# The mixer's output projection by seven products in two chunks

## The chip, the cores and the metric

One core of one Trainium2 chip. The metric is the device time of one execution in microseconds (us), the median over the runs shown, lower is better.

## The reference

One inference step of one hybrid layer, for a prompt of 512 tokens and 8 single sampled tokens, 520 columns in all; everything is float32. What matters here:

```
proj = rmsnorm(x, g_mix) @ w_in          # 2048 -> 6160 columns
ya   = bg * causal_dwconv(cg * hin)      # short convolution: 1024 features
yb   = norm(gla(q, k, v, gate)) * silu(og)   # 4 linear-attention heads: 1024 features
x1   = x + concat([ya, yb]) @ w_out      # 2048 x 2048, the output projection
u, v = split(rmsnorm(x1, g_ffn) @ w_up)  # 2048 -> 2 * 5632
h    = silu(causal_dwconv(u) + b) * v
x2   = x1 + h @ w_down                   # 5632 x 2048
y    = rmsnorm(x2, g_final)
```

## The kernel before, in words

Activations lie with features on the 128 partitions and the T = 520 tokens along the row, in two halves of HT = 260. A float32 operand is split into a rounded part hi (ScalarE, a copy into fp32r) and a rest lo = raw - hi (VectorE), and every product is three matmuls: hi by hi, hi by lo and lo by hi. Weights are streamed from DRAM as 512 KB pieces `raw` of 128x1024, by DMAs on the queue of SP (SyncE), and split the same way into `hi` and `lo`.

The order of work:

1. *Input projection.* Tiles of 128 output columns. `group()` issues, for one tile, 16 rows of weights x 3 x 2 halves of matmuls (L134). Eight tiles of the mixer's convolution branch (`conv_tile`), then four attention heads, and eight tiles of its output gate. Each finished tile of 128 mixer outputs is split into yh and yl, which stay in SBUF (`ym`).
2. *Output projection* (`projected`, `kept`, L914 to L1003). 16 tiles, again by `group()`, in pairs (k, k+8). To each the residual from `xT_d` is added, the result goes to DRAM (`x1_d`), its squares are added up on GpSimd (POOL) in `ssq`, and, multiplied by the norm's weight, it becomes one of the quarters of the FFN's input. From a pair, `quarter_sums` forms four sums of quarters, `t21` and `t34`; these go to DRAM (`t_d`). During the last pair, whose two tiles are interleaved, they come back on SP's queue, and `sums_parts` splits them in place of the mixer's outputs that are no longer needed.
3. *FFN up*, 44 tiles t, and *FFN down*, 5 chunks c of 1024 features x 4 groups g of 512 outputs; the last 512 features are done in the ordinary way. Both use a scheme of seven products in place of the eight quarter products of a 2x2 block multiplication. Each product takes a weight piece or a sum of weight pieces, and a quarter of the input or a sum of quarters (the "input forms"). One product is 24 matmuls of 128x128 by 128x260 in both.
4. Final norm.

Step 3's two stages share one loop over `order`, a list of (kind, where, product): seven products j = 0..6 per tile or group. At each product the loop issues the matmuls, and puts what other engines must do at fixed points of it: `begin(n)` asks for three of the next group's four weight pieces at j = 0, `load_rest` for the fourth at j = 2; `prepare(i + 2)` makes hi and lo (L1093 on ScalarE, L1097 on VectorE) for the product two further on, and a sum of weights (`plus`, L1048, in a single tile `s` that is updated in place: pieces 22 + 21, then + 11, then + 12). The sum for product 7 is an adding DMA from SBUF to SBUF (`seventh`, L1062, the rows raw<-raw) on POOL's queue at j = 5. Steps such as `gate(t)`, which turns a finished up tile into h, are generators: each `yield` says how many products after its start the next part is issued. Engines run their instructions in this order of issue, and so do the DMA queues of SP and POOL.

The FFN's norm factor R (one number per token) is computed from `ssq` at the third product of the first up tile, whose products stand in an order of their own, with more PSUM banks (`BANK0`). The other tiles take R in when PSUM is emptied (`up_finish`).

In the down-projection the input forms of chunk c are read from DRAM (`f_d`, written by `gate`) by `load_form(c, j)`, four DMAs of 128x2x260 for each of the seven products; the forms for chunk 0 are asked for in the last up tile at j = 4 (four products' worth) and in the first down group at j = 0 (three). The residual x1 is read into `acc` (`load_residual`, at j = 6 of the last up tile for group 0). The share of the fifth product that two accumulators need is kept in `h5` and added by POOL in the last chunk.

## Time and profile before

| | |
|---|---|
| Time, median of 3 runs | 2246.64 us (2244.97 to 2248.2) |
| The profiled execution: its own time | 2249.65 us |
| its span, first to last instruction | 2247.9 us |
| TensorE (PE) busy | 2206.9 us, 98% of the span, 18147 matmuls |
| VectorE (DVE) busy | 1559.2 us, 69% |
| ScalarE (ACT) busy | 997.4 us, 44% |
| GpSimd (POOL) busy | 406.6 us, 18% |
| Transfers | 377.09 MB, 168 GB/s on average |
| Mean granted TensorE clock | 0.993 |

All rows but the first come from one profiled execution, and durations in the text are its durations. "Busy" counts the time in which at least one instruction of the engine ran; since matmuls are pipelined, a single matmul's duration (some 283 ns) is longer than the distance from one to the next. The busy share is a mean over the stages named above, which have quite different loads; the stage of the output projection lies at about 688 to 876 us of the span, FFN up at 876 to 1768, and FFN down from there on.

### The profile page before, as it was taken

What the parts mean: (1) busy time and instruction counts of PE and PEld (TensorE: products, weight loads), DVE (VectorE), ACT (ScalarE), POOL (GpSimd) and SP (SyncE); (2) the same over time, 40 slices, a digit from 0 to 9 for tenths busy, and PEclk for the clock granted to TensorE, in tenths of its full rate; (3) what the DMA queues carried; (4) which work ended last, traced back from release to release, by engine and by line L of the source; (5) the groups of instructions that cost most, each with busy time, mean ns of one, the idle gap of its engine ahead of it and who ended that gap; (6) DMA issues with size and microseconds to landing.
All of it is one profiled execution on the core that took longest, in us unless ns stands there. A gap on an engine that the chain in (4) does not pass through costs nothing.

```text
span 2247.9 us, 43792 instructions
## 1 busy us (share of the span) xinstructions
PE 2206.9 (98%) x18147; PEld 2183.9 (97%) x18147; DVE 1559.2 (69%) x2081; ACT 997.4 (44%) x1417; POOL 406.6 (18%) x539
## 2 busy tenths in 40 slices
PE   8999999999999999999999999999999999999997
PEld 6999999999999998999999999999999999999997
DVE  5355363544334547888889888898888767777876
ACT  5334334312222335555555555555555444444445
POOL 3023132210001222111311122112122400000310
PEclk9999999999999999999999999999999999999999
DMA  8243334333444556576776767667676987876944
GB/s 247 83 132 102 111 113 114 99 104 86 109 118 137 163 159 203 151 188 159 184 186 175 185 165 188 177 172 179 175 187 191 302 239 212 264 212 186 285 120 151
DMA packets 459395, 377.09 MB, mean 168 GB/s; under 512 B 19081, under 2 KB 423461, under 8 KB 459053
## 3 DMA queue, kind: packets, MB, share of 16 engines
q1 hardware_dynamic: 429585, 280.03, 43.6%
q0 software_dynamic: 28288, 92.05, 15.7%
q8 instruction: 142, 2.33, 0.4%
q10 hardware_dynamic: 1324, 2.23, 0.3%
q14 instruction: 56, 0.46, 0.1%
HBM read 278.15 MB, written 63.27 MB: 152 GB/s over the span
## 4 chain that ended last, share of the span: by engine, by line
PE 83%; issue 7%; DMA 4%; DVE 3%; POOL 2%; ACT 1%; SPq 0%; ACTq 0%; POOLq 0%; DVEq 0%
PE mm L134 32%; PE mm L1125 22%; PE ms L1125 9%; PE y L1312 6%; PE x L1312 6%; PE f L1312 2%; PE e L1312 2%; PE ms L753 1%; DMA raw<-raw 1%; POOL f_d L1192 1%; DMA raw<-in_w_in_dram 0%; PE ms L739 0%; PE tp L284 0%; DVE lo L106 0%; DVE lo L1097 0%
## 5 line engine op out<-in xcount | busy, mean ns | idle before, releaser
L1125 PE MATMUL mm<-yl,hi 128*128 128x260 f32 x1408 | 398.8, 283 | 0.0
L1125 PE MATMUL mm<-yh,hi 128*128 128x260 f32 x1408 | 397.9, 283 | 0.0
L1125 PE MATMUL mm<-yh,lo 128*128 128x260 f32 x1408 | 397.3, 282 | 0.0
L1093 ACT ACTIVATE hi<-raw 128x1024 fp32r<-128x1024 f32 x256 | 270.7, 1057 | 205.9 <-issue 72.4
L1097 DVE TENSOR_TENSOR lo<-raw,hi 128x1024 fp32r<-128x1024 f32 x256 | 318.6, 1245 | 53.9 <-ACT hi L1093 52.5
L105 ACT ACTIVATE hi<-raw 128x1024 fp32r<-128x1024 f32 x144 | 152.0, 1056 | 394.4 <-PE mm L134 378.5
L134 PE MATMUL mm<-xh,hi 128*128 128x260 f32 (+2 forms) x1280 | 314.1, 294 | 10.1 <-ACT xh L120 5.7
L106 DVE TENSOR_TENSOR lo<-raw,hi 128x1024 fp32r<-128x1024 f32 x144 | 185.6, 1289 | 183.9 <-ACT hi L105 173.6
L1097 DVE TENSOR_TENSOR lo<-s,hi 128x1024 fp32r<-128x1024 f32 x192 | 238.0, 1239 | 101.1 <-ACT hi L1093 95.9
L134 PE MATMUL mm<-xh,lo 128*128 128x260 f32 (+2 forms) x1280 | 302.0, 285 | 0.7 <-DVE lo L106 0.7
L134 PE MATMUL mm<-xl,hi 128*128 128x260 f32 (+2 forms) x1280 | 299.7, 283 | 1.5 <-DVE xl L121 1.4
L1093 ACT ACTIVATE hi<-s 128x1024 fp32r<-128x1024 f32 x192 | 202.8, 1056 | 177.8 <-DVE s L1048 58.2
L1125 PEld LDWEIGHTS mm<-yh,lo 128*128 128x128 f32 x1408 | 265.5, 189 | 0.0
L1125 PEld LDWEIGHTS mm<-yl,hi 128*128 128x128 f32 x1408 | 265.0, 188 | 0.0
L1125 PEld LDWEIGHTS mm<-yh,hi 128*128 128x128 f32 x1408 | 264.6, 188 | 0.0
L134 PEld LDWEIGHTS mm<-xh,hi 128*128 128x128 f32 x1280 | 216.5, 190 | 20.3 <-issue 7.7
L134 PEld LDWEIGHTS mm<-xl,hi 128*128 128x128 f32 x1280 | 216.4, 190 | 2.3 <-DVE xl L121 2.3
L134 PEld LDWEIGHTS mm<-xh,lo 128*128 128x128 f32 x1280 | 215.0, 189 | 1.1 <-DVE lo L106 1.1
L1125 PE MATMUL ms<-xh,hi 128*128 128x260 f32 x704 | 199.9, 284 | 2.8 <-ACT xh L117 2.8
L1125 PE MATMUL ms<-xh,lo 128*128 128x260 f32 x704 | 199.7, 284 | 0.0
L1125 PE MATMUL ms<-xl,hi 128*128 128x260 f32 x704 | 199.1, 283 | 0.5 <-DVE xl L118 0.5
L1062 POOL DMA_DIRECT2D raw<-raw x63 | 56.4, 895 | 594.5 <-DVE s L1048 503.5
(397 smaller groups left out, 5242.9 us busy)
## 6 DMA issues: line engine op xcount, KB each, us to landing
raw<-in_w_up_dram SPq DMA_DIRECT2D x176, 512.0 KB
raw<-in_w_down_dram SPq DMA_DIRECT2D x96, 512.0 KB
raw<-in_w_in_dram SPq DMA_DIRECT2D x92, 512.0 KB
form<-f_d SPq DMA_DIRECT2D x126, 260.0 KB
raw<-raw POOLq DMA_DIRECT2D x63, 512.0 KB, 5.5
f_d<-t POOLq DMA_DIRECT2D x80, 260.0 KB, 5.5
raw<-in_w_out_dram SPq DMA_DIRECT2D x28, 512.0 KB
f_d<-fh POOLq DMA_DIRECT2D x40, 260.0 KB, 4.9
```

The source lines that it names most:

```text
L105: nc.scalar.activation(hi, raw, AF.Copy)
L106: nc.vector.tensor_tensor(lo, raw, hi.bitcast(F32), op=ALU.subtract)
L134: nc.tensor.matmul(o, w, xx, start=first and i == 0, stop=last and i == 2)
L753: nc.tensor.matmul(pb[:, c * 64 : (c + 1) * 64], L[:, c, :], rhs[:, c], start=True, stop=True,)
L1062: nc.gpsimd.dma_start(raw[2, 1], raw[1, 1], accum_op=ALU.add)
L1093: nc.scalar.activation(his[i], src, AF.Copy)
L1097: nc.vector.tensor_tensor(los[i], src, his[i].bitcast(F32), op=ALU.subtract)
L1125: nc.tensor.matmul(st["bank"][b], w[:, k, :], x, start=b not in st["used"] and k == 0 and j == 0, stop=k == 7 and j == 2, skip_group_check ...
L1192: nc.gpsimd.dma_start(d, x)
L1312: nc.tensor.matmul(ps[:, m, :], w[:, k, m * P : (m + 1) * P], x, start=b not in st["used"] and k == 0 and j == 0, stop=k == 3 and j == 2, ...
```

## The change

The output projection joins the loop of seven products. `order` now begins with 2 chunks c x 4 groups g of kind "wo": chunk c stands for half of the 2048 mixer features, group g for 512 of the 2048 outputs, and `chunk_product` and `chunk_finish` (before: `down_product`, `down_finish`) serve them as they serve the down-projection.

- *Its inputs.* A mixer tile isn't split on its own: with every second tile (`mixed_done`) the sums of quarters are made (`pair_sums`), and four tiles are split and stored to DRAM (`g_d`) as hi and lo, by eight DMAs on POOL's queue (`stored`). `load_form("wo", c, j)` reads them back on POOL's queue: chunk 0 during the last output-gate tiles, chunk 1 mostly during the last group of chunk 0.
- *Its results* are added up in `acc`, into which `load_residual` first reads the residual from `xT_d`.
- *The FFN's inputs.* In chunk 1, the group's four accumulators become final during the group. `projected(g)` then stores them (`ready`, to `x1_d`, on SP's queue), scales them, squares them (`square`; the sums `ssq` are adding DMAs on POOL's queue), and makes quarters and sums of quarters, split into place (`form`) or, for groups 0 to 2 and the forms 4, 5 and 6, into temporary tiles and from there to `t_d` (`out`, on SP's queue), whose home still holds inputs of the output projection. `load_sum` reads these back on SP's queue in the last group.
- *Weight sums.* In chunk 1 the third sum of a group is an adding DMA as well (`dma_plus`, with `dma[3]` issued at j = 0).
- *R* is computed in the second up tile, from `norm_sums`; the first two up tiles have it multiplied in afterwards, and `gate(0)` starts five products later. All up tiles now use one order of products.
- *Down.* The fifth product's share goes directly into the accumulators at r = 6 (`onto`), and `h5` is gone. The forms for chunk 0 are asked for in the last up tile at j = 1, 2, 4 and 6, and the residual at j = 5.
- Pools: the tiles of the input in SBUF are laid out in pairs (`pair_tiles`), and the weight pieces of the second column have a pool of their own (`raw2`).

```diff
+    g_d = [dp.tile([7, 2, 4, P, HT], F32, name=f"g_d{c}") for c in range(2)]
+    t_d = dp.tile([3, 4, 2, P, T], F32, name="t_d")
...
+    def load_form(kind, c, j):
+        home = (7 * c + j) % 8
+        parts_ = []
+        for x in range(2):
+            tiles = []
+            for q in range(2):
+                t = slots[2 * home + q].tile(
+                    [P, T], F32R, tag=f"y{'hl'[x]}{2 * home + q}", name="form"
+                )
+                first = kind == "wo" or c == 0 and x == 1
+                (nc.gpsimd if first else nc.sync).dma_start(
+                    two(t.bitcast(F32)),
+                    forms_d[kind][c][PLACE[ORDER[j]], x, 2 * q : 2 * q + 2].rearrange(
+                        "i p c -> p i c"
+                    ),
+                )
+                tiles += halves(t)
+            parts_.append(tiles)
+        xd[kind, c, ORDER[j]] = list(zip(*parts_))
+    def stored(src, dst, hi):
+        hi = hi[:, : src.shape[1]]
+        split(src, hi.bitcast(F32R), src.bitcast(F32R))
+        for d, x in zip(dst, (hi, src)):
+            if len(d.shape) == 3:
+                x = two(x)
+                d = d.rearrange("f p c -> p f c")
+            nc.gpsimd.dma_start(d, x)
+    def pair_sums(he, h):
+        t21, t34 = tmp()[:, :T], tmp()[:, :T]
+        (b11, b12), (b21, b22), (t2, t1), (t3, t4) = map(halves, (he, h, t21, t34))
+        sub(t1, b11, b12)
+        minus(t2, t1, b22)
+        sub(t3, b22, b12)
+        minus(t4, t2, b21)
+        return t21, t34
...
+        def mixed_done(k, y):
+            if k % 2 == 0:
+                return
+            he, dst, i = even.pop(k - 1), g_d[k // 8], k // 2 % 4
+            t21, t34 = pair_sums(he, y)
+            for src, f in ((halves(he)[0], 6), (t21, 0), (t34, 2), (y, 4)):
+                n = 1 if f == 6 else 2
+                stored(src, [dst[f : f + n, x, i] for x in range(2)], tmp())
...
+            if 2 <= j < 6:
+                for x in range(2 * j - 4, min(2 * j - 2, 7)):
+                    load_form("wo", 0, x)
...
-        def kept(m, xt):
-            nc.gpsimd.dma_start(x1_d[m], xt[:, :T])
-            if m == 0:
-                nc.scalar.activation(ssq, xt[:, :T], AF.Square)
-            else:
-                sq = tmp()
-                nc.scalar.activation(sq[:, :T], xt[:, :T], AF.Square)
-                ptt(ssq, ssq, sq[:, :T], ALU.add)
...
-        for k in range(LK):
-            for m in (k, k + 8):
-                xt = tmp()
-                nc.sync.dma_start(xt[:, :T], xT_d[m])
-                projected(m, group(w_out, m * P, ya), xt)
-                kept(m, xt)
-            t21, t34 = tmp()[:, :T], tmp()[:, :T]
-            quarter_sums(k, t21, t34)
-            nc.gpsimd.dma_start(t_d[k], t21)
...
-                if k % 8 < LK:
-                    load_sums(k)
...
+        def dma_plus(out, x):
+            return lambda: nc.gpsimd.dma_start(out, x, accum_op=ALU.add)
...
+        sums = {5: plus(s, raw[2, 2], raw[2, 1]), 6: plus(s, s, raw[1, 1])}
+        dma = {}
+        if state:
+            dma[7] = dma_plus(raw[2, 1], raw[1, 1])
+        else:
             sums[7] = plus(raw[2, 1], raw[2, 1], raw[1, 1])
-        def seventh():
-            nc.gpsimd.dma_start(raw[2, 1], raw[1, 1], accum_op=ALU.add)
-        return dict(src=src, sums=sums, bank={}, used=set(), rest=loads[3], seventh=seventh)
...
+    groups = [("wo", (c, g)) for c in range(2) for g in range(NG)]
+    groups += [("up", (t,)) for t in range(NF)]
+    groups += [("down", (c, g)) for c in range(NCD) for g in range(NG)]
+    order = [(*x, r) for x in groups for r in ORDER]
+    NW = 7 * 2 * NG
+    NU = NW + 7 * NF
...
+        if r == 2 and t < 2:
+            nc.scalar.activation(z1, bk["e"], AF.Copy)
         elif r == 2:
             nc.vector.tensor_tensor(z1, bk["e"], R[:, :HT], op=ALU.mult)
-        elif r == 7:
-            add(v2, bk["a"], st["c"])
         elif r == 3:
             add(z2, bk["f"], st["c"])
-            nc.vector.tensor_tensor(z2, z2, R[:, HT:], op=ALU.mult)
-        elif r == 4:
...
+        d = 0 if t else 5
+        yield d
+        nc.vector.tensor_tensor(v[:, :T], v[:, :T], R, op=ALU.mult)
+        yield d + 0.5
+        if t < 2:
+            nc.vector.tensor_tensor(z[:, 2 : 2 + T], z[:, 2 : 2 + T], R, op=ALU.mult)
         c = tmp()
...
-                ptt(acc[g, 1], acc[g, 1], h5[g], ALU.add)
-                ptt(acc[g, 3], acc[g, 3], h5[g], ALU.subtract)
+        if r == 6:
+            onto(1, "c")
+            onto(3, "c", ALU.subtract)
...
+    def form(f, g):
+        if f == 1:
+            x = pair_tiles(bigA, f"b{g}")
+        elif f in (2, 3):
+            x = [
+                bigA.tile([P, T], F32R, tag=acc_tag(4 * g + q), name="b2")
+                for q in ((0, 3) if f == 2 else (1, 2))
+            ]
+        else:
+            k = {5: 0, 4: 4, 6: 8, 7: 12}[f] + g
+            x = [slots[k].tile([P, T], F32R, tag=f"y{s}{k}", name=f"y{s}{k}") for s in "hl"]
+        for j, q in enumerate(zip(*(halves(y) for y in x))):
+            xq[f, 2 * g + j] = q
+        return x
+    def projected(g):
+        xg = {}
+        def ready(q):
+            a, m = acc[g, q], first_tile("wo", g, q // 2)
+            nc.sync.dma_start(rows_of(x1_d, "wo", g, q), two(a))
+            xg[q] = tmp()[:, :T]
+            for j in range(2):
+                nc.scalar.activation(
+                    halves(xg[q])[j], halves(a)[j], AF.Copy, scale=gffn[:, m + j : m + j + 1]
+                )
+        def square(q):
+            if g == 0 and q in (0, 3):
+                nc.scalar.activation(ssq[q % 2], acc[g, q], AF.Square)
+                return
+            sq = fh()
+            nc.scalar.activation(sq, acc[g, q], AF.Square)
+            nc.gpsimd.dma_start(ssq[q % 2], sq, accum_op=ALU.add)
+        def out(f, t):
+            if f == 7 or g == NG - 1:
+                split(t, *form(f, g))
+            else:
+                hi = tmp()[:, :T]
+                split(t, hi.bitcast(F32R), t.bitcast(F32R))
+                for d, x in zip((t_d[f - 4, g, 0], t_d[f - 4, g, 1]), (hi, t)):
+                    nc.sync.dma_start(d, x)
+        yield 4.5
+        ready(0)
+        split(xg[0], *form(1, g))
+        yield 5.5
+        ready(3)
+        square(0)
+        yield 6.5
+        ready(1)
+        square(3)
+        yield 7
+        t1, t2 = xg[0], tmp()[:, :T]
+        sub(t1, xg[0], xg[1])
+        minus(t2, t1, xg[3])
+        yield 7.5
+        ready(2)
+        out(5, t1)
+        yield 8
+        t4 = tmp()[:, :T]
+        minus(t4, t2, xg[2])
+        yield 8.5
+        out(4, t2)
+        out(7, t4)
+        yield 9
+        square(1)
+        split(xg[2], *form(2, g))
+        t3 = xg[1]
+        sub(t3, xg[3], xg[1])
+        yield 9.5
+        out(6, t3)
+        yield 10.5
+        square(2)
+        yield 11
+        split(xg[3], *form(3, g))
+    def load_sum(f, g):
+        for x, d in zip(form(f, g), (t_d[f - 4, g, 0], t_d[f - 4, g, 1])):
+            nc.sync.dma_start(x.bitcast(F32), d)
...
+            if kind == "wo" and at[0] == 1:
+                steps.append([projected(at[1]), i, 0])
...
+        if j == 0 and 3 in state[kind, at]["dma"]:
+            state[kind, at]["dma"][3]()
+        if j == 5 and more:
+            state[groups[n + 1]]["dma"][7]()
...
-        if i == 2:
-            factors = rsqrt_rest(rsqrt_sums(ssq), D, R)
-        if i in (3, 4):
+        if i == NW + 7:
+            factors = rsqrt_rest(norm_sums(), D, R)
+        if i in (NW + 8, NW + 9):
             next(factors)
-        if kind == "up" and n == NF - 1:
-            if j == 4:
-                for x in range(4):
-                    load_form(0, x)
-            if j == 6:
-                load_residual(0)
+        if kind == "wo":
+            c, g = at
+            if c == 0 and g == 0 and j == 0:
+                load_form("wo", 1, 0)
+            if c == 0 and j == 4 and g + 1 < NG:
+                load_residual("wo", g + 1)
+            if c == 0 and g == NG - 1 and j >= 1:
+                load_form("wo", 1, j)
+            if c == 1 and g == NG - 1:
+                for f, h in {
+                    1: ((5, 0), (5, 1)), 2: ((5, 2),), 3: ((4, 0), (4, 1)), 4: ((4, 2),),
+                    5: ((6, 0), (6, 1)), 6: ((6, 2),),
+                }.get(j, ()):
+                    load_sum(f, h)
+        if kind == "up" and at[0] == NF - 1:
+            for x in {1: (0, 1), 2: (2, 3), 4: (4, 5), 6: (6,)}.get(j, ()):
+                load_form("down", 0, x)
+            if j == 5:
+                load_residual("down", 0)
...
-            if c == 0 and g == 0 and j == 0:
-                for x in (4, 5, 6):
-                    load_form(0, x)
...```

What this does to the order of instructions, at three places. First VectorE. Before, in the output projection, while the next to last pair's results are finished (mm is what the matmuls left in PSUM, t a temporary tile, xl the rest of a split quarter, lo the rest of a weight piece):

```order
L106 TENSOR_TENSOR lo<-raw,hi 128x1024
L924 TENSOR_TENSOR t<-mm,t 128x260 x2
L106 TENSOR_TENSOR lo<-raw,hi 128x1024
L917 TENSOR_TENSOR t<-t 128x260
L919 TENSOR_TENSOR t<-t 128x260
L118 TENSOR_TENSOR xl_8102<-t,xh_8101 128x520
L918 SCALAR_TENSOR_TENSOR t<-t 128x260
L920 SCALAR_TENSOR_TENSOR t<-t 128x260
```

and after, in a group of the second chunk (acc<-acc,y is an accumulator's update, s a weight sum):

```order
L1032 TENSOR_TENSOR s<-s,raw 128x1024
L1263 TENSOR_TENSOR acc<-acc,y 128x520
L589 TENSOR_TENSOR t<-t 128x520
L583 SCALAR_TENSOR_TENSOR t<-t 128x520
L1087 TENSOR_TENSOR lo<-s,hi 128x1024
L118 TENSOR_TENSOR t<-t 128x520
L583 SCALAR_TENSOR_TENSOR t<-t 128x520
L1087 TENSOR_TENSOR lo<-raw,hi 128x1024
L118 TENSOR_TENSOR t<-t 128x520
L118 TENSOR_TENSOR yl_9172<-t,yh_9171 128x520
L118 TENSOR_TENSOR b_9204<-t,b_9203 128x520
```

Between two weight pieces there now stand accumulators' updates, weight sums and several sums and splits of the FFN's inputs, where one pair's sums and one split stood.

Second, SP's queue at the end of the output projection. Before, the last weights of w_out, the first of w_up, and then the sums of quarters from DRAM:

```order
L983 DMA raw<-in_w_out_dram 128x4x128 x2
L1045 DMA raw<-in_w_up_dram 128x8x128 x3
L1076 DMA raw<-in_w_up_dram 128x8x128
L978 DMA t<-xT_d 128x520 x2
L955 DMA t<-t_d 128x520 x12
```

and after:

```order
L1308 DMA x_d<-acc 128x2x260 x3
L1029 DMA raw<-in_w_up_dram 128x8x128 x3
L1308 DMA x_d<-acc 128x2x260
L1331 DMA t_d<-t 128x520 x4
L1369 DMA yh_9461<-t_d 128x520
L1369 DMA yl_9462<-t_d 128x520
L1369 DMA yh_9465<-t_d 128x520
L1369 DMA yl_9466<-t_d 128x520
L1066 DMA raw<-in_w_up_dram 128x8x128
L1331 DMA t_d<-t 128x520 x2
```

The stores of the results and of the sums of quarters have moved onto this queue, between the weights and ahead of the loads of the same sums.

Third, POOL's queue where the down-projection begins. Before, the forms for chunk 0 (on this queue the half with x = 1, the lo parts), with the adding copy of weights between them:

```order
L1266 DMA form<-f_d_9504 128x2x260 x8
L1062 DMA raw<-raw 128x1024
L1280 DMA acc<-x_d 128x2x260 x4
L1266 DMA form<-f_d_9504 128x2x260 x6
L570 DMA out_dram<-flat 11x128 x10
L1192 DMA hh_d_9515<-fh 128x520
L1192 DMA hl_d_9516<-t 128x520
```

and after:

```order
L612 DMA form<-f_d_7543 128x2x260 x8
L630 DMA hh_d_7552<-fh 128x520
L630 DMA hl_d_7553<-t 128x520
L612 DMA form<-f_d_7543 128x2x260 x4
L1036 DMA raw<-raw 128x1024
L1220 DMA acc<-x_d 128x2x260 x4
L612 DMA form<-f_d_7543 128x2x260 x2
L574 DMA out_dram<-flat 11x128 x10
L630 DMA hh_d_7554<-fh 128x520
```

Twelve forms instead of eight stand ahead of the copy, but the first eight are issued two to three products earlier, and a store of the last tiles' h stands between them.

More of the change, by code (lines that the diff above doesn't have):

```diff
@@ L1072, in begin @@
         kind, at = groups[n]
-        state[at] = weights(up_source if kind == "up" else down_source, *at)
+        state[kind, at] = weights(source(kind, at), kind == "wo" and at[0] == 1)
     def load_rest(n):
-        nc.sync.dma_start(*state[groups[n][1]]["rest"])
+        nc.sync.dma_start(*state[groups[n]]["rest"])
     def prepare(i):
@@ L1242, in gate, with fh @@
         yield 14
-        stored(h, [dst[4:6, x, i] for x in range(2)])
+        stored(h, [dst[4:6, x, i] for x in range(2)], fh())
+    def fh():
+        return wxp.tile([P, T], F32, tag="fh", name="fh")
     f_d = [dp.tile([7, 2, 4, P, HT], F32, name=f"f_d{c}") for c in range(NCD)]
+    forms_d["down"] = f_d
     hl_d = [[dp.tile([P, T], F32, name=f"h{s}_d{t}") for s in "hl"] for t in range(CH)]
@@ L1351, in down_finish @@
             onto(2, "a", ALU.subtract)
+    ssq = [cp.tile([P, T], F32, tag="glr", name="ssq"), R]
+    def form(f, g):
[6 more added lines that the diff above has]
+            ]
+        else:
+            k = {5: 0, 4: 4, 6: 8, 7: 12}[f] + g
[3 more added lines that the diff above has]
+        return x
@@ L1355, in run_steps, with norm_sums @@
+    def load_sum(f, g):
+        for x, d in zip(form(f, g), (t_d[f - 4, g, 0], t_d[f - 4, g, 1])):
+            nc.sync.dma_start(x.bitcast(F32), d)
+    def norm_sums():
+        pss = []
+        for b in range(2):
+            pss.append(bank())
+            for j, x in enumerate(halves(ssq[b])):
+                nc.tensor.matmul(pss[b][:, :HT], ones, x, start=j == 0, stop=j == 1)
+        return pss
     def run_steps(now):
@@ L1380, in trunk_kernel @@
             seeded = {b: two_banks(b) for b in "ef"}
[L1381 to L1389 removed]
+        elif i == NW:
+            mmp = pctx.enter_context(tc.tile_pool(name="mm", bufs=4, space=PSUM))
+            msp = pctx.enter_context(tc.tile_pool(name="misc", bufs=4, space=PSUM))
@@ new lines, in trunk_kernel @@
+        (up_product if kind == "up" else chunk_product)(i)
+        if j == 0:
+            if n and groups[n - 1][0] == "up":
+                steps.append([gate(groups[n - 1][1][0]), i, 0])
+            if kind == "wo" and at[0] == 1:
+                steps.append([projected(at[1]), i, 0])
+        run_steps(i)
+        if i in (0, NU):
+            marked(seeded["e"], xd[kind, 0, 1][0][0])
+        if i in (2, NU + 2):
+            marked(seeded["f"], xd[kind, 0, 1][0][0])
+        if i == NW:
+            x = xq[1, 0][0]
+            for ps in [bank() for _ in range(4)]:
+                nc.tensor.matmul(ps[:, :HT], x[:, :P], x, start=True, stop=True)
```

356 lines of the change are left out of this document (117 added, 239 removed).

## The prediction, made before the changed kernel was run

> **What bounds the kernel now.** I read the page's parts 1 and 2 first, then the same stretches as a table by stage, then the groups of instructions.
>
> ```profile
> PE 2206.9 (98%) x18147; PEld 2183.9 (97%) x18147; DVE 1559.2 (69%) x2081; ACT 997.4 (44%) x1417; POOL 406.6 (18%) x539
> ...
> PEclk9999999999999999999999999999999999999999
> DMA  8243334333444556576776767667676987876944
> ```
>
> TensorE is busy for 98% of the span at full clock; nothing else is near that. So time goes only where matmuls go, or where TensorE starts to wait. The stages (columns: start:end, length, then busy us and count for PE, PEld, DVE, ACT, POOL, then PEclk, DMA share, GB/s) show how much room the other engines have:
>
> ```profile
> 600.00:684.00 84.00, 84.00 (x701) 84.00 (x700) 32.26 (x43) 24.39 (x29) 0.00 (x0) 1.00 0.41 115
> 690.00:840.00 150.00, 150.00 (x1252) 150.00 (x1251) 69.24 (x89) 48.00 (x65) 30.48 (x37) 1.00 0.51 160
> 920.00:1720.00 800.00, 800.00 (x6674) 800.00 (x6673) 710.43 (x953) 434.34 (x641) 157.84 (x227) 1.00 0.68 177
> 1840.00:1870.00 30.00, 30.00 (x253) 30.00 (x252) 21.95 (x22) 13.05 (x15) 0.87 (x1) 1.00 1.05 327
> 1870.00:1900.00 30.00, 30.00 (x253) 30.00 (x252) 22.79 (x24) 12.65 (x14) 1.71 (x2) 1.00 0.68 188
> ```
>
> The rows are the end of the input projection, the output projection, the FFN's up-projection and two pieces of its down-projection. 1252 matmuls in 150 us are 119.8 ns each; that pitch is the same in all five. VectorE at 89% (row three) and the transfers at 1.05 and 327 GB/s (row four) are the highest loads that still cost TensorE nothing. There are two places where it does wait, the crossing from the output projection into the FFN and that from up to down:
>
> ```profile
> 872.00:880.00 8.00, 4.67 (x24) 4.28 (x23) 7.97 (x15) 5.38 (x10) 4.73 (x4) 0.79 0.37 115
> ...
> 892.00:896.00 4.00, 1.97 (x17) 1.79 (x16) 3.55 (x6) 1.76 (x2) 3.83 (x3) 1.00 0.62 159
> ```
>
> ```profile
> 1760.00:1770.00 10.00, 8.35 (x58) 7.95 (x57) 8.84 (x12) 3.62 (x5) 8.13 (x12) 0.87 1.01 348
> 1770.00:1780.00 10.00, 10.00 (x82) 10.00 (x81) 3.88 (x4) 5.57 (x9) 5.08 (x9) 0.96 1.06 322
> 1780.00:1790.00 10.00, 9.08 (x76) 8.87 (x75) 8.57 (x10) 3.71 (x4) 7.33 (x14) 1.00 1.07 353
> 1790.00:1800.00 10.00, 10.00 (x85) 10.00 (x85) 5.54 (x6) 3.22 (x4) 6.36 (x9) 1.00 1.07 352
> 1800.00:1810.00 10.00, 7.83 (x51) 7.42 (x50) 4.85 (x6) 4.25 (x5) 0.00 (x0) 0.83 1.02 319
> ```
>
> At 119.8 ns, 12 us hold 100 matmuls; the first pair of rows has 41, so 59 are missing: 7.1 us. 50 us hold 417; the second table has 352: 65 x 0.1198 = 7.8 us.
>
> **The change part by part.** *Matmuls.* The output projection is 16 tiles x 16 rows of weights x 3 x 2 halves:
>
> ```profile
> L134 PE MATMUL mm<-yh,hi 128*128 128x260 f32 x512 | 103.5, 284 | 0.0
> L134 PE MATMUL mm<-yh,lo 128*128 128x260 f32 x512 | 103.3, 283 | 0.0
> L134 PE MATMUL mm<-yl,hi 128*128 128x260 f32 x512 | 102.6, 281 | 0.0
> ...
> L517 PE MATMUL ms<-ssq,ones 128*128 128x260 f32 x4 | 1.0, 382 | 0.0
> ```
>
> That is 1536. After: 2 chunks x 4 groups x 7 products x 24 = 1344, of the same shape. 192 fewer x 0.1198 = **-23.0 us**. Four marking matmuls (0.5 us) and two more sums over ssq are added (today's two are the four records of L517, 1.0 us): **+1.5**.
>
> *The old crossing.* The 59 matmuls were missing because the last two tiles' split, sums and t_d loads stood on VectorE (busy 7.97 of 8 us) with TensorE waiting, and then for R's factors. After, the inputs of the first FFN tile come with each group, and the first two tiles do without R: **-7.1** for what goes; what comes in its place is priced next.
>
> *VectorE in the second chunk.* From the groups (mean ns), and the timeline, where ops that follow each other start closer than their durations:
>
> ```profile
> L1097 DVE TENSOR_TENSOR lo<-raw,hi 128x1024 fp32r<-128x1024 f32 x256 | 318.6, 1245 | 53.9 <-ACT hi L1093 52.5 <-DMA form<-f_d 1.4
> L1048 DVE TENSOR_TENSOR s<-s,raw 128x1024 f32<-128x1024 f32 x128 | 156.6, 1223 | 2.2
> L118 DVE TENSOR_TENSOR yl<-t,yh 128x520 fp32r<-128x520 f32 x32 | 21.8, 695 | 11.4 <-ACT yh L117 11.3
> L1326 DVE TENSOR_TENSOR acc<-acc,e 128x520 f32<-128x520 f32 x20 | 13.9, 693 | 0.9
> ```
>
> ```profile
> 865.80 1.91 DVE L118 TENSOR_TENSOR yl<-t,yh 128x520 fp32r<-128x520 f32 x3
> 867.63 1.22 DVE L1048 TENSOR_TENSOR s<-raw 128x1024 f32<-128x1024 f32 x1
> ...
> 884.94 1.21 DVE L1097 TENSOR_TENSOR lo<-raw,hi 128x1024 fp32r<-128x1024 f32 x1
> 886.07 1.21 DVE L1048 TENSOR_TENSOR s<-s,raw 128x1024 f32<-128x1024 f32 x1
> ```
>
> So 1.13 us apart for the wide ones, 0.61 (1.83 / 3) for 520 columns. A group of the second chunk has 7 lo and 2 weight sums (9 x 1.13 = 10.2), 6 additions onto acc, 4 input sums and 7 splits (17 x 0.61 = 10.4): 20.6 us, against 168 x 0.1198 = 20.1 for TensorE. Over four groups it falls 2 us behind; weights are made two products (5.8 us) ahead, so this may cost nothing (low end 0). By the full durations it is 9 x 1.24 + 17 x 0.69 = 22.9, so 4 x 2.8 = 11 (high end). The pitch was seen on this engine in full flow, so I stand near it but add a little for its waits on ScalarE: **+3**. ScalarE's share is smaller:
>
> ```profile
> L1093 ACT ACTIVATE hi<-raw 128x1024 fp32r<-128x1024 f32 x256 | 270.7, 1057 | 205.9 <-issue 72.4 <-PE mm L1125 61.1 <-PE x L1312 19.6
> L117 ACT ACTIVATE yh<-t 128x520 fp32r<-128x520 f32 x32 | 19.9, 636 | 29.8 <-DVE t L603 10.4 <-DVE t L900 10.4 <-DMA t<-t_d 7.8
> L1179 ACT ACTIVATE t<-mm 128x260 f32<-128x260 f32 x43 | 16.7, 389 | 80.4 <-PE mm L1125 80.4
> ```
>
> 7 x 1.06 + 13 x 0.64 (7 splits, 4 squares, 2 copies) + 8 x 0.39 = 18.9 of 20.1: full, but not over, and its overlap is not counted.
>
> *Transfers in the second chunk.* Sizes are from the list of DMA issues:
>
> ```profile
> raw<-raw POOLq DMA_DIRECT2D x63, 512.0 KB, 5.5
> f_d<-fh POOLq DMA_DIRECT2D x40, 260.0 KB, 4.9
> x_d<-t POOLq DMA_DIRECT2D x16, 260.0 KB, 2.4
> t_d<-t POOLq DMA_DIRECT2D x14, 260.0 KB, 3.6
> ```
>
> A middle group moves four weight pieces (2.1 MB), two adding copies raw<-raw (1.05), 4 x1_d stores, 4 adding copies onto ssq and 6 t_d stores (14 x 0.266 = 3.7): 6.9 MB. The first has no t_d and no ssq copies yet but 2.5 MB left of the 24 form loads issued in the group before: 6.4. In the last group and the five FFN products until the last t_d tile is used, 12 products or 34.5 us, it is 18 t_d loads (4.8), the weights and copies of two groups and what is left of the stores: 12 MB. Together 6.4 + 6.9 + 6.9 + 12 = 32.2 MB in 3 x 20.1 + 34.5 = 94.8 us. At 353 GB/s (row 1780) that takes 91 us: nothing (low end). At 188 / 0.68 x 1.07 = 295, which is row 1870's mix of weights, copies and forms run at the share's top, 109: +14 (high end). The mix lies between, with more plain 260 KB pieces than row 1870, so I take 325: 99 us, **+4.3**. The waiting places: t_d loads stand on SP's queue behind t_d and x1_d stores that wait for VectorE and ScalarE, and ahead of the next weights, which have 20 us in hand; ScalarE's split into a new tmp waits for a t_d store two products old (landing 3.6 us where nothing was crowded, so 2 us spare); the third weight sum is now a POOL copy behind the form loads, with three products for its 5.5 us.
>
> The Trainium skill, *DMA: Bandwidth & Descriptors*, section "Specifications", gives about 358 GB/s as the HBM limit of a core. The busiest row here, 353, agrees. Copies from SBUF to SBUF (7.4 of the 32.2 MB) would not count there, so by the page the stretch would need an estimated 69 us, the term would be 0 and the sum 4.3 us lower.
>
> *Mixer and start of the projection.* A pair of tiles gets four small sums, two more splits, 8 stores of 1.9 MB on POOL. At 600 to 684 VectorE is at 38%, ScalarE at 29%, transfers at 115 GB/s, POOL empty: hidden; earlier POOL also runs the heads' steps, and 8 issues (some 0.6 us each) can delay one. The first chunk's forms load during the last tiles; the first three products' weights are ready before these end. On VectorE the evacuation, four sums and four splits of the last pair then stand between weights: about 8 us for what must be ready in 8.6. Between 0 and one product (2.9): **+0.5**. The adding copies replace 15 additions on POOL, each free before.
>
> *R's factors* come in the second FFN tile; between 0 and the 2 us lost at 892 to 896: **+1**.
>
> *The crossing to the down-projection.* Now the forms load from the second product of the last FFN tile on, not from the fifth, some 8.6 us earlier, and no longer ahead of the adding copy of weights in one lump. The chain of waits shows what was late:
>
> ```profile
> 1767.66 9.37 DMA raw<-raw
> 1779.25 6.51 DMA form<-f_d
> 1786.04 5.11 DMA out_dram<-flat
> 1794.56 7.86 DMA raw<-raw
> ```
>
> The bytes are the same and the second group's copy still stands behind forms, ten small stores and residuals, so not all of the 7.8 us goes: ends -7.8 and 0, I take **-4**. One addition more per down group (0.61 us in rows with VectorE at 73 to 76%) is hidden; so are eight POOL additions that go.
>
> **Sum.** -23.0 + 1.5 - 7.1 + 3 + 4.3 + 0.5 + 1 - 4 = -23.8. The profiled execution took 2249.65 us (span 2247.9 and 1.75 around it): 2225.85. It lies 3.0 above the median of the runs, 2246.64, against which I predict: 2222.85, said as **2223**.
>
> **The rivals.** (1) *The second chunk is bound by its transfers* (slower). Row 920 to 1720, with weights, one adding copy per tile and form stores, moved 177 GB/s at a share of 0.68: 260 at a full share. If doubled adding copies hold it to 250, 32.2 MB take 129 us, 34 more than TensorE instead of 4.3: 2223 + 30 = 2253. It decides from about 262 GB/s downwards, where the sum is zero. For it: the adding copies are a fifth of the bytes, and no row shows them this dense. Against: weights come here in pieces twice as wide as in that stage, and 1840 to 1870 reached 327 without loss. (2) *VectorE sets the pace*, by full durations and each of its waits on ScalarE: +11 instead of +3, so 2231. For it: VectorE is above the 89% that is known to be free. Against: the pitch. (3) *The transfers never bind*, 353 GB/s holding at both places: terms 4.3 and -4 become 0 and -7.8, 2215. This is what the Trainium skill's limit above gives for the first of the two. For it: the 30 us at 327. Against: 1800 to 1810, where one late copy cost 34 matmuls, 4 us. (4) *No change*: several of these terms at middling values, 2242 to 2251. That the matmuls are not removed is excluded: the program has 190 rows fewer on TensorE.
>
> **How the numbers follow.** Forecast 0.55 (2216 to 2234 by itself), (1) 0.10, (2) 0.15, (3) 0.15, (4) 0.05. Low end: all of (3) and no VectorE loss, 2211 or so; high end: (2) with the transfers at 295, 2223 + 8 + 10 = 2241, and a little of (4): 2244. That leaves out (1) and the edges of (3) and (4), under 0.2. 0.2% (4.5 us) is about what a measurement of this kernel can tell from no change. Faster by more: forecast, (2), (3), 0.85; within: 0.05; slower: 0.10.
>
> **What would show it.** In the new profile, 8 groups of 20.1 us at pitch 119.8 ns in the output projection; VectorE close to full in the second half of it; GB/s above 300 there; the first FFN tile without a hole like 872 to 880; the crossing to down with fewer than 65 missing matmuls. I am wrong if matmuls in the second chunk come in under 150 per 20 us, or if the hole of the old crossing is back under another name, such as a split waiting for a t_d load.

## The result, and the profile after

2262.64 us, median of 4 runs (2257.99 to 2263.39), against 2246.81 for the kernel before: 15.8 us slower, ratio 1.0067, 95% interval 1.0049 to 1.0084. I had forecast 2223 and a range of 2211 to 2244. The profiled execution took 2262.26 us, its span is 2260.6, 12.7 above before.

Parts 1 and 2 of the page after:

```profile
PE 2195.8 (97%) x17963; PEld 2172.9 (96%) x17963; DVE 1631.3 (72%) x2188; ACT 1039.6 (46%) x1486; POOL 461.4 (20%) x640
...
PE   8999999999999977999999999999999999999997
...
DMA  8343354374787789476676766667666987876944
GB/s 249 84 126 105 107 156 113 87 210 121 201 248 242 219 233 299 126 195 174 167 195 160 194 173 178 183 160 193 174 180 191 308 236 218 258 205 195 282 122 151
```

There are 184 fewer matmul records (192 matmuls fewer for the projection, 8 more for sums and markings), and yet TensorE's share of the longer span is lower: two slices at 7 tenths, from about 790 to 905 us, where before stood 9. By stage (after, then the same stretches before; a 25 us stretch without gaps has 210 records, since a stretch also counts those that overlap its ends):

```profile
690.00:770.00 80.00, 80.00 (x667) 80.00 (x666) 63.51 (x66) 33.74 (x37) 32.84 (x46) 1.00 0.84 254
770.00:795.00 25.00, 21.02 (x151) 20.51 (x150) 14.66 (x18) 11.90 (x19) 3.78 (x5) 0.86 0.64 178
795.00:930.00 135.00, 109.92 (x837) 108.40 (x836) 93.16 (x111) 78.37 (x121) 24.95 (x26) 0.90 0.90 243
930.00:1720.00 790.00, 787.57 (x6572) 787.29 (x6572) 703.66 (x946) 428.90 (x632) 154.06 (x221) 1.00 0.67 176
```

```profile
770.00:795.00 25.00, 25.00 (x210) 25.00 (x210) 10.92 (x14) 8.26 (x11) 4.95 (x6) 1.00 0.51 160
795.00:930.00 135.00, 129.65 (x1060) 128.94 (x1059) 91.23 (x117) 63.08 (x89) 27.95 (x26) 0.99 0.59 173
```

The first chunk (row 690) loses nothing. From 770 to 930, the second chunk and the start of the FFN, there are 988 matmuls against 1270 before: 282 missing, 33.8 us more than before. A further 2.4 us is lost in row 930, where before had none: VectorE multiplies R into the second up tile afterwards, a step of ScalarE waits for that, and behind this step stands the copy of a PSUM bank that TensorE needs. That is nearly the whole result: -23.0 for the products, +33.8 and +2.4 here, about 13 against the spans' 12.7 (changes of 1 us and less are left out).

Who waited, in that stretch, by the lists of waits of TensorE and ScalarE (total us, times, longest):

```profile
PE y L1249 <- ACT f L1269: 11.2, 2, 6.1
PE x L1249 <- ACT f L1269: 7.4, 1, 7.4
```

```profile
ACT t L117 <- DMA t_d<-t: 26.7, 3, 10.1
```

and the same on ScalarE's and SP's timelines and on the chain of waits:

```profile
798.95 1.04 ACT L1083 ACTIVATE hi<-raw 128x1024 fp32r<-128x1024 f32 x1
807.80 0.64 ACT L117 ACTIVATE t<-t 128x520 fp32r<-128x520 f32 x1 [7.82 <-DMA t_d<-t]
808.35 0.59 ACT L1269 ACTIVATE f<-y 128x520 f32<-128x520 f32 x1
```

```profile
791.07 3.17 SPq L1029 DMA_DIRECT2D raw<-in_w_out_dram  x3
794.33 1.19 SPq L1308 DMA_DIRECT2D x_d<-acc  x1
795.61 3.76 SPq L1331 DMA_DIRECT2D t_d<-t  x4
799.47 0.42 SPq L1066 DMA_DIRECT2D raw<-in_w_out_dram  x1
```

```profile
763.45 9.97 DMA form<-g_d
...
773.98 7.76 DMA s<-raw
...
799.06 9.23 DMA t_d<-t
...
826.60 11.57 DMA t_d<-t
...
877.18 10.85 DMA x_d<-acc
...
894.03 7.06 DMA x_d<-acc
```

Five holes, and a transfer at the start of each. The split for sum 6 needs a ninth temporary tile out of a ring of eight, and gets that of sum 5. The store of that tile is the first of the four t_d stores in SP's row. It left at 795.6, just after ScalarE had made the tile, with three pieces of weights and a store of x1 still on their way ahead of it. The semaphore on which the split waits was full 12.1 us later, and the split starts at 807.8. (The chain's rows name the last of the four stores instead, 799.06 and 826.60, and so show 9.23 and 11.57.) In the next two groups this store took 12.7 and 8.0 us. ScalarE stands still for it three times, with the copy of a PSUM bank (`f`) behind it, for which TensorE waits. The first hole begins with the adding copy s<-raw behind the form loads on POOL's queue, the last with the split that overwrites an accumulator: it waits for the store of x1, which stands among 18 loads of sums. After each hole the granted clock is low for a while:

```profile
785.00:790.00 5.00, 5.00 (x26) 5.00 (x26) 4.48 (x6) 4.54 (x8) 0.86 (x1) 0.54 0.31 107
790.00:795.00 5.00, 5.00 (x45) 5.00 (x44) 4.93 (x7) 3.59 (x8) 0.01 (x1) 1.00 0.91 199
```

26 matmuls instead of 44 in a fully busy 5 us: 18 x 0.12, another 2.2 us for this hole. (The Trainium skill, *TensorE: Matmul & The Clock Gate*, "What's actually happening", has the clock at half after an idle window of some 3.4 us; the rows agree, 0.54 after a hole of about 4 us.)

### The profile page after: what moved, and what is told of

Read it like the earlier page. It is cut to its first block, busy times and chain, and to the rows that moved or that the text cites. A ratio compares the mean times of both kernels' runs of the same rounds, so it can differ in the third digit from the quotient of the medians.

```text
span 2260.6 us, 43939 instructions
## 1 busy us (share of the span) xinstructions
PE 2195.8 (97%) x17963; PEld 2172.9 (96%) x17963; DVE 1631.3 (72%) x2188; ACT 1039.6 (46%) x1486; POOL 461.4 (20%) x640
## 2 busy tenths in 40 slices
PE   8999999999999977999999999999999999999997
DMA  8343354374787789476676766667666987876944
## 4 chain that ended last, share of the span: by engine, by line
PE 88%; DMA 6%; DVE 3%; ACT 1%; POOL 1%; issue 1%; SPq 0%; ACTq 0%; DVEq 0%; POOLq 0%
PE mm L1108 27%; PE mm L134 25%; PE ms L1108 11%; PE y L1249 8%; PE x L1249 8%; PE f L1249 3%; PE e L1249 3%; PE ms L830 1%; DMA t_d<-t 1%; DMA form<-g_d 1%; DMA x_d<-acc 1%; DVE lo L1087 1%; DMA raw<-in_w_down_dram 0%; DMA acc<-x_d 0%; PE ms L1516 0%
## 5 line engine op out<-in xcount | busy, mean ns | idle before, releaser
L1083 ACT ACTIVATE hi<-raw 128x1024 fp32r<-128x1024 f32 x288 | 304.4, 1057 | 225.7 <-issue 79.5
L1108 PE MATMUL mm<-yh,hi 128*128 128x260 f32 x1408 | 398.6, 283 | 2.8 <-ACT ms L1118 2.4
L1108 PE MATMUL mm<-yl,hi 128*128 128x260 f32 x1408 | 397.8, 283 | 0.0
L1108 PE MATMUL mm<-yh,lo 128*128 128x260 f32 x1408 | 397.5, 282 | 0.0
L1087 DVE TENSOR_TENSOR lo<-raw,hi 128x1024 fp32r<-128x1024 f32 x288 | 351.3, 1220 | 57.7 <-ACT hi L1083 57.6
L1087 DVE TENSOR_TENSOR lo<-s,hi 128x1024 fp32r<-128x1024 f32 x216 | 265.3, 1228 | 111.0 <-ACT hi L1083 105.6
L1083 ACT ACTIVATE hi<-s 128x1024 fp32r<-128x1024 f32 x216 | 228.4, 1057 | 223.9 <-DVE s L1032 92.6
L1108 PEld LDWEIGHTS mm<-yh,hi 128*128 128x128 f32 x1408 | 265.1, 188 | 3.3 <-ACT ms L1118 2.6
L1108 PEld LDWEIGHTS mm<-yl,hi 128*128 128x128 f32 x1408 | 265.9, 189 | 0.0
L1108 PEld LDWEIGHTS mm<-yh,lo 128*128 128x128 f32 x1408 | 265.8, 189 | 0.1
L1108 PE MATMUL ms<-b,hi 128*128 128x260 f32 x1408 | 256.6, 282 | 4.6 <-DVE b L118 4.6
L106 DVE TENSOR_TENSOR lo<-raw,hi 128x1024 fp32r<-128x1024 f32 x112 | 144.4, 1290 | 138.1 <-ACT hi L105 131.5
L1108 PEld LDWEIGHTS ms<-b,hi 128*128 128x128 f32 x1408 | 217.1, 188 | 4.8 <-DVE b L118 4.8
L1249 PE MATMUL y<-form,hi 128*128 128x260 f32 x1120 | 210.7, 288 | 11.2 <-ACT f L1269 11.2
L1249 PE MATMUL x<-form,hi 128*128 128x260 f32 x1120 | 208.4, 286 | 9.2 <-ACT f L1269 7.4
L1036 POOL DMA_DIRECT2D raw<-raw x71 | 63.5, 895 | 700.1 <-DVE s L1032 585.2
L1108 PE MATMUL ms<-b,lo 128*128 128x260 f32 x704 | 198.5, 282 | 0.0
L1249 PEld LDWEIGHTS y<-form,hi 128*128 128x128 f32 x1120 | 177.6, 193 | 11.6 <-ACT f L1269 11.6
L1249 PEld LDWEIGHTS x<-form,hi 128*128 128x128 f32 x1120 | 175.5, 191 | 10.0 <-ACT f L1269 7.6
L1032 DVE TENSOR_TENSOR s<-s,raw 128x1024 f32<-128x1024 f32 x140 | 170.9, 1221 | 2.5
L1249 PE MATMUL y<-form,lo 128*128 128x260 f32 x560 | 161.3, 288 | 3.8 <-DVE lo L1087 3.8
```

The source lines that it names most:

```text
L106: nc.vector.tensor_tensor(lo, raw, hi.bitcast(F32), op=ALU.subtract)
L1032: return lambda: nc.vector.tensor_tensor(out, x, y, op=ALU.add)
L1036: return lambda: nc.gpsimd.dma_start(out, x, accum_op=ALU.add)
L1083: nc.scalar.activation(his[i], src, AF.Copy)
L1087: nc.vector.tensor_tensor(los[i], src, his[i].bitcast(F32), op=ALU.subtract)
L1108: nc.tensor.matmul(st["bank"][b], w[:, k, :], x, start=b not in st["used"] and k == 0 and j == 0, stop=k == 7 and j == 2, skip_group_check ...
```

## Experiments

Two theories stood at the start. **Theory 1, places**: the transfers have room (252 GB/s on average from 765 to 905), and each hole is one wait in an unlucky place. **Theory 2, bytes** (the prediction's first rival): the second chunk asks for more than the transfers give, so a hole that is mended opens elsewhere. Medians of before, run beside each set of them, were 2246.2 to 2246.8; ratios are against before.

**The wait for the temporary tile.**

```
-    hi = tmp()[:, :T]
+    hi = zpad[g % 2][:, 2 : 2 + T] if f == 6 else tmp()[:, :T]     # in out()
```

> The hi part of sum 6 of groups 0 to 2 goes into a tile that is free there (zpad) instead of the next one of the eight temporary tiles, so ScalarE no longer waits for a store of sum 5. Theory 1 (one wait in the wrong place; the transfers have room, 240 GB/s on average in the second chunk): ScalarE's three waits of 7.8, 10.1 and 8.8 us are gone, TensorE gets back most of the 57 + 79 + 74 = 210 missing matmuls, 25 us: about 2238. Theory 2 (bound by bytes, the first rival): the same holes come back as waits for weights or for the next store: 2255 to 2263.

2253.43 (1.0029, 1.0019 to 1.0039): 9 us of the 25 came back. The three waits for t_d are gone from ScalarE's list (a single one of 1.2 us is left), and another is now on it:

```profile
ACT hi L1083 <- DMA s<-raw: 17.1, 4, 7.2
```

```profile
795.00:930.00 135.00, 114.53 (x880) 109.90 (x879) 100.84 (x124) 83.54 (x129) 24.92 (x26) 0.97 0.91 247
```

43 matmuls more than the changed kernel in this stretch, where theory 1 wants 210. Neither theory's number is met; theory 2's is missed by less.

**The stores on another queue.**

```
-    nc.sync.dma_start(d, x)
+    nc.gpsimd.dma_start(d, x)                                      # in out(), t_d
```

> The stores of the sums (t_d) go by POOL's queue instead of SP's, temporary tiles as they are. If the store lands after 9 to 12 us because it stands behind three weight pieces and x1 stores in SP's own queue, it lands in 5 us or less on the other queue and the three holes shrink by 15 to 25 us: 2238 to 2248. If it is late because all queues share the same sixteen engines and these are full (1.0 to 1.09), it lands as late and the time stays at 2258 to 2265.

2259.76 (1.0057, 1.0037 to 1.0078), 2.9 us less than the changed kernel, inside the uncertainty. By the list of DMA issues the stores still take 9.7 us at the median to land:

```profile
t_d<-t POOLq DMA_DIRECT2D x18, 260.0 KB, 9.7
```

ScalarE's waits for them went all the same: the split for sum 6 starts at 799.4, before any store of its group has landed, so it found another tile free; why, this run does not tell. Waits for the copy s<-raw took their place:

```profile
ACT hi L1083 <- DMA s<-raw: 17.3, 4, 5.9
```

They are as long as in the first experiment, where the stores were not on POOL's queue. So changing the queue does not buy time here: the queues share what is full. (The Trainium skill, *DMA: Bandwidth & Descriptors*, "Issuing engines are not separate DMA queues", says that all issuers' transfers run on the same 16 engines; the 9.7 us agrees.)

**The first and the last hole.**

```
-    state[kind, at] = weights(source(kind, at), kind == "wo" and at[0] == 1)
+    state[kind, at] = weights(source(kind, at), kind == "wo" and at[0] == 1 and at[1] > 0)
```

> The third weight sum of group 0 of the second chunk is added by VectorE again (groups 1 to 3 keep the adding DMA). Theory 1 (that copy alone was late, since it stood behind the 24 form loads on POOL's queue): the hole at 775 to 790, 57 matmuls or 6.9 us, goes, and one addition of 1.1 us on VectorE is hidden: about 2256. Theory 2 (bound by bytes): the hole moves to another wait: 2260 to 2263.

2257.07 (1.0043, 1.0026 to 1.0060): 5.6 less, theory 1's number. The hole is gone and stays gone:

```profile
770.00:795.00 25.00, 25.00 (x211) 25.00 (x210) 20.46 (x24) 17.23 (x27) 4.62 (x7) 1.00 0.76 214
```

```
-    nc.sync.dma_start(rows_of(x1_d, "wo", g, q), two(a))
+    (nc.gpsimd if g == NG - 1 else nc.sync).dma_start(rows_of(x1_d, "wo", g, q), two(a))
```

> In the last group the four stores of x1 go by POOL's queue instead of SP's, where they stand among 18 loads of sums. Theory 1 (the split that overwrites the accumulator waits for the store, and the store for its place in the queue): the hole at 895 to 905, 51 matmuls or 6.2 us, goes: about 2256.5. Theory 2 (the transfers are full there, 300 GB/s and more, so the store lands late on any queue): 2260 to 2264.

2258.61 (1.0056, 1.0041 to 1.0071): 4.0 less, between the two. From 890 to 910 there are 141 matmuls instead of 112, which is 3.5 us. The intervals of these last two runs overlap that of the changed kernel (1.0049 to 1.0084), so the times alone do not carry the two gains; the matmuls in the mended stretches are the better witness.

**Bytes alone.** The first experiment without the adding copies onto ssq in groups 1 to 3, for which neither a matmul nor a weight waits (ScalarE waited 1.5 us for one of them in the first experiment):

```
-    nc.gpsimd.dma_start(ssq[q % 2], sq, accum_op=ALU.add)
+    if g == 0:
+        nc.gpsimd.dma_start(ssq[q % 2], sq, accum_op=ALU.add)
```

> As the first experiment (own tile for sum 6), and the adding copies onto ssq are left out for groups 1 to 3, so R is made from group 0 alone: 12 copies of 266 KB, 3.2 MB, are not moved. No matmul and no weight waits for them. Theory 1 (what is left after the first experiment are further single waits in queues): no change, 2251 to 2256. Theory 2 (bound by bytes; from 795 to 895 the transfers stood at a share near 1.07 and 290 GB/s): 3.2 MB / 290 = 11 us less: about 2242.

2244.02 (0.9988, 0.9979 to 0.9998): 9.4 us less than the first experiment. This speaks for theory 2: nothing is gained but room. It is not that the weight sums now stand in a shorter queue of POOL: ScalarE's waits for s<-raw are 16.6 us here, 17.1 in the first experiment.

```profile
795.00:930.00 135.00, 124.64 (x961) 122.33 (x961) 110.10 (x135) 89.78 (x139) 14.60 (x14) 0.95 0.84 236
```

**Bytes, or the adding?** The same copies, overwriting:

```
-    nc.gpsimd.dma_start(ssq[q % 2], sq, accum_op=ALU.add)
+    nc.gpsimd.dma_start(ssq[q % 2], sq)
```

> As the first experiment (own tile for sum 6), but the 14 copies onto ssq overwrite instead of adding, so R is made from the last squares alone; bytes and queue are the same. Leaving 12 of them out saved 9.4 us. If an adding copy takes the engines about twice as long as a plain one (between the first experiment and the one without these copies, POOL's queue moved 2.2 MB less in 14.8 us less of sixteen engines' time, 151 GB/s, where SP's queue moves 317), this saves about half: 2248 to 2250. If only the bytes count: 2252 to 2255.

2248.77 (1.0013, 1.0004 to 1.0022): 4.7 less than the first experiment, half of what leaving them out gave. By the ratios it is 3.6 us, and the two intervals overlap a little, so the time alone is a weak witness. The DMA queues of the stretch 765 to 905 (MB, then the share of sixteen engines in 140 us) say the same. The changed kernel:

```profile
q1 hardware_dynamic: 25196, 24.22, 54.6%
q0 software_dynamic: 4074, 10.96, 37.5%
```

POOL's queue of the first experiment, with plain copies, and without 12 of them:

```profile
q0 software_dynamic: 4198, 11.42, 38.9%
```

```profile
q0 software_dynamic: 3248, 11.22, 31.0%
```

```profile
q0 software_dynamic: 2759, 9.18, 28.3%
```

From 38.9 to 31.0% are 11.1 us of all sixteen engines; one form load fell out of the stretch as well (0.84 at 317 GB/s), so 14 copies cost 0.73 us more each when they add. From 38.9 to 28.3% are 14.8 us; three form loads came into the stretch (2.5), so 12 adding copies took 17.3, or 1.44 us each: 266 KB at 185 GB/s, against 0.71 us for a plain one. Over the wider stretch 690 to 930, in which the form loads all lie, the three shares are 39.5, 34.6 and 32.3%, and the same working gives 1.5 and 0.7. An adding copy takes the transfer engines twice as long.

**Fewer bytes for the sums.**

```
     # out(): the sum is stored as it is
-    hi = tmp()[:, :T]
-    split(t, hi.bitcast(F32R), t.bitcast(F32R))
-    for d, x in zip((t_d[f - 4, g, 0], t_d[f - 4, g, 1]), (hi, t)):
-        nc.sync.dma_start(d, x)
+    nc.sync.dma_start(t_d[f - 4, g, 0], t)
     # load_sum(): one load, and 3.5 products later the split in place
+    hi, lo = form(f, g)
+    nc.sync.dma_start(lo.bitcast(F32), t_d[f - 4, g, 0])
+    def later():
+        yield 3.5
+        split(lo.bitcast(F32), hi, lo)
```

> The sums go to t_d unsplit, one store and one load each, and are split into place 3.5 products after the load: 9 stores and 9 loads of 266 KB fewer, 4.8 MB, and no temporary tile for the hi part, so ScalarE's waits for t_d go as in the first experiment. Nine splits move from the first three groups into the last group and the first FFN tile. Theory 1: as the first experiment, 2253, or up to 3 us more for the splits that now stand late. Theory 2: 4.8 MB / 290 = 16 us less than that: about 2237 to 2241.

2247.72 (1.0004, 0.9994 to 1.0015): 5.7 less than the first experiment, where theory 2 wanted 12 to 16 and theory 1 nothing. The hole at 770 to 795 was still there (164 records).

**All places.** With the first experiment's tile, the store of x1 in the last group by POOL, and no adding copy for the third weight sum (VectorE adds it in all four groups):

```
-    state[kind, at] = weights(source(kind, at), kind == "wo" and at[0] == 1)
+    state[kind, at] = weights(source(kind, at), False)
```

> Own tile for sum 6, no adding DMA for the third weight sum in any group (VectorE adds it), and x1 of the last group by POOL's queue. Theory 1: the single gains add, 9 + 5.5 + 4: about 2244. Theory 2: beyond that 3 more copies of 512 KB are not moved, and ScalarE's waits for them (17 us in the first experiment) go: 2235 to 2240. If VectorE is the bound of the second chunk (the second rival), four additions cost 4.5 us and eat most of it: 2244 to 2249.

2238.67 (0.9959, 0.9944 to 0.9974): 24.0 below the changed kernel, where the three single gains add to 18.8 (9.2 + 5.6 + 4.0). The other 5 us come with three more copies that are not moved and with ScalarE's waits for them, which are gone; this run does not tell the two apart. And the same with the unsplit sums:

> Unsplit sums, no adding DMA for the third weight sum, x1 of the last group by POOL's queue. Theory 2 (bytes): 4.8 MB of stores and loads and 2.1 MB of copies fewer than in the changed kernel, all three places open: 2225 to 2232. If VectorE is the bound instead: its 4 additions and the late splits keep it at 2236 to 2242.

2231.95 (0.9931, 0.9916 to 0.9946): 14.3 us faster than before, 30.7 faster than the change as it came.

```profile
770.00:840.00 70.00, 70.00 (x584) 70.00 (x583) 67.01 (x79) 52.80 (x81) 11.94 (x14) 1.00 0.95 254
840.00:860.00 20.00, 11.95 (x82) 11.59 (x81) 16.21 (x21) 12.14 (x21) 5.65 (x7) 0.83 1.09 316
860.00:930.00 70.00, 67.57 (x556) 67.05 (x555) 57.74 (x73) 44.38 (x66) 11.08 (x11) 1.00 0.57 144
```

In the first row VectorE is busy for 67.0 of 70 us, and TensorE loses nothing. One hole is left, in the second row, where the last group ends and the FFN begins. To see if it is the late load before a split:

```
-        yield 3.5
+        yield 5 if f == 5 else 4.5
```

> As the kernel with all three places open and unsplit sums (2232), but the splits of the loaded sums are issued 4.5 to 5 products after the load instead of 3.5. There the only hole left in the output projection (840 to 860, about 93 matmuls) begins with a split that waits for a load that takes 8.5 us. If that wait alone makes the hole: 2222 to 2226. If the first FFN tile then waits for the splits themselves or for the transfers: 2228 to 2233.

2230.71 (0.9932, 0.9918 to 0.9946): the same within 1.2 us. The hole is smaller, but not gone:

```profile
840.00:870.00 30.00, 25.40 (x195) 24.80 (x194) 28.88 (x38) 23.22 (x40) 7.35 (x9) 0.94 1.10 304
```

Here VectorE is busy for 28.9 of 30 us and the transfers are at 1.10. The chain of waits says which of the two set the end in this run: from 835.5 to 849.8 it goes from one of VectorE's operations to the next, splits of the loaded sums among them, with no transfer in it.

```profile
834.92 0.60 ACT f L1269
835.52 1.22 DVE lo L1087
...
849.06 0.70 DVE acc L1263
849.76 0.14 issue
849.90 4.54 PE mm L1108 x24
```

So taking the late load out of the way put VectorE in its place.

**The crossing to the down-projection.** The new times for its first loads alone, on the kernel before; and the old times on the best kernel so far:

```
 # in the last up tile
-    if j == 4:  load_form(0, 0..3)      j == 6: load_residual(0)      # 4, 5, 6 in the first group
+    for x in {1: (0, 1), 2: (2, 3), 4: (4, 5), 6: (6,)}.get(j, ()): load_form(0, x)
+    if j == 5:  load_residual(0)
```

> The kernel before with the changed kernel's times for the first loads of the down-projection (forms at j = 1, 2, 4, 6 of the last up tile, residual at j = 5) and nothing else. My prediction's term for this was -4 (ends -7.8 and 0): about 2242.5. If the stretch is bound by its bytes (share 1.0 to 1.09 for 50 us in both kernels), moving the loads by 8 us inside it changes little: 2245 to 2248.

> As the kernel with all three places open and unsplit sums (2232), but with the kernel before's times for the first loads of the down-projection. If my term of -4 was right: 2236. If that stretch is bound by its bytes: 2231 to 2233.

2247.42 (1.0004, 0.9996 to 1.0012) and 2233.37 (0.9940, 0.9927 to 0.9953; 1.4 above the same kernel with the new times). On the kernel before, a gain of 4 is excluded. On the best kernel the 1.4 us are within what the runs can tell (some 3 us either way), so that run alone would leave the question open. The stretch 1765 to 1850 of before, after and the first of these two:

```profile
1765.00:1850.00 85.00, 80.26 (x636) 79.35 (x636) 56.02 (x58) 36.50 (x45) 27.18 (x40) 0.96 0.90 276
```

```profile
1765.00:1850.00 85.00, 80.15 (x641) 79.56 (x640) 62.57 (x69) 34.00 (x41) 29.29 (x44) 0.96 0.90 280
```

```profile
1765.00:1850.00 85.00, 79.68 (x647) 79.08 (x648) 57.17 (x60) 36.68 (x45) 23.10 (x35) 0.98 0.92 280
```

In the chain of waits of after, the late transfer here is no longer the adding copy, but the weights of the second down group, which SP issued from 1786.5 on, behind the form loads:

```profile
1791.35 10.52 DMA raw<-in_w_down_dram
```

One queue order was exchanged for another with the same end. That it is the bytes (share 1.01 to 1.09 for 50 us) fits, but no run took bytes out of this stretch.

## Why the prediction was wrong

The forecast that came nearest was the first rival's, 2253, to which I gave 0.10. Its cause, adding copies that take the engines twice, was there. But it priced no waits, and its 250 GB/s came about (252 on average) in part because the transfers stood still in between. By the steps:

- *Matmuls, -23.0*: right. Row 690 to 770 has the same number at the same pitch as before, and 184 records fewer in all.
- *The old crossing, -7.1*: its cause went, but the stretch from 770 to 930 that replaced it lost 33.8 more than the old one. My own test for being wrong ("the hole of the old crossing is back under another name") came true with the store of x1. So did the other one: 837 matmuls in the 135 us from 795 on are 124 per 20 us, where I had set 150.
- *Transfers in the second chunk, +4.3, ends 0 and +14*: **the step that failed**, in its rate, and in the waiting places that it named and put at nothing.
  - *The rate.* I took 325 GB/s for the mix. From 765 to 905, SP's queue moved 24.22 MB in 54.6% of 140 us, 317 GB/s, and POOL's 10.96 MB in 37.5%, 209: together 273 at a share of 1. The rates between which I chose were for shares of 1.05 to 1.07. At 1.07 the 273 are 292, about the 295 that I had worked out from row 1870 as the high end, and my 32.2 MB need 110 us instead of 99, 15 over the 94.8 that were there. (The 32.2 are also 0.3 short: the parts of the first group's 6.4 MB add up to 6.7.) The reason is the adding copy, which occupies the engines twice. Of the 35.3 MB in that stretch 8.4 were adding copies (nine of 512 KB, raw<-raw and s<-raw, and fourteen of 260 KB onto ssq). Row 1870 had them nearly as dense (1.05 of 5.65 MB), row 1840 hardly (0.52 of 9.81 MB), and yet I took a rate close to that of the second. The trace of before held another hint: in the up stage the adding copy is about a seventh of the bytes (0.52 of 3.6 MB per tile), and the rate at a full share was 260. I worked that out in the first rival, and did not use it in the sum.
  - *The waiting places.* With the measured rate alone the sum would have been 2234, or 2242 at a share of 1, which is inside my range. By the experiments most of the other 21 to 29 us are the waits of the next two points and of the last store of x1, for which my sum has no term; 4 are the crossing to down (below). One by one the three places gave 9.2, 5.6 and 4.0 us, together and with three copies fewer 24.0. After the holes the transfers are not full either: the share is 0.64 and 0.62 from 810 to 820, 0.60 and 0.62 from 840 to 850, and from 780 to 790 they stood nearly idle (0.17, 56 GB/s). There SP's queue waited 11.6 us for an accumulator before the stores of x1, and the weights and stores behind it then came in one burst. How much that adds no run measured by itself.
- *The landing of the stores*: in the same step I named the wait of ScalarE's split for a store "two products old" and gave it 2 us to spare, from a landing of 3.6 us "where nothing was crowded". In this stage the landing was 12.1, 12.7 and 8.0 us, and the waits 7.8, 10.1 and 8.8. The store was not two products (5.8 us) old either: it had left 4.4 and 3.0 us before the split wanted the tile, and the third time had not left yet. A landing time measured in an empty stage was used for a full one. The first experiment puts this wait at 9 us of the time, out of the 25 that its three holes cost. That the other 16 stay lost to the bytes behind it is what theory 2 says, and the 9.4 us of the run without the adding copies speak for it, but no run shows all 16.
- *The third weight sum* "with three products for its 5.5 us": 9.1 us at the median, and for group 0 behind the form loads. Giving that one sum back to VectorE brought 5.6 us.
- *VectorE, +3, and the second rival*: wrong in the other direction for most of the chunk. With all places open, at 67.0 of 70 us busy, it cost nothing, the low end of my range: its operations overlap at the pitch I had read (1.13 and 0.61 us), and two products in hand cover the rest. The second rival is refuted for the first three groups. At the end of the last it holds, once the late load is out of the way: there the chain is VectorE's work alone.
- *Mixer and start, +0.5*: 8 or 9 matmuls are missing from 600 to 684 (692 records for 701), 1.0 us.
- *R, +1*: 2.4.
- *The crossing to down, -4*: no gain on the kernel before, 2247.42 where the term wanted 2242.5, and none on the best kernel that the runs can tell; the end of 0 was right as far as they show.

Had the three waits been absent and the sums stored unsplit, the forecast would have been 9 us off (2231.95 for 2223): 4 of them are the crossing to down; the others were not taken apart.

## What to carry to other kernels

Before a term of transfers is summed, sort its bytes by kind: an adding copy counted here double, and a mix of kinds has no single rate. Compare rates at the same share of the engines' time. Take the landing time of a transfer from a stage as full as the one it will stand in, and ask who holds a buffer until it lands: a ring of eight tiles with nine users per round put ScalarE, then TensorE, behind a store that nobody reads soon. Here a mended wait showed its full worth only when the resource behind it had room; to learn that, leave out transfers for which nobody waits.
